# Embedding gate of a decoder block as seven products of halves, with weight sums and half of the output additions done by transfers

## The chip, the core and the metric

The kernel runs on one core of a Trainium2 chip. The engines named below are PE (TensorE, the matrix products), DVE (VectorE), ACT (ScalarE), POOL (GpSimd, which also issues DMA transfers from its own queue) and SP (SyncE, which issues most DMA transfers). The metric is the device time of one execution in microseconds (us), as the median of several runs.

## The reference, cut to what matters

The model is one decoder layer on 512 tokens of width 1024 in float32. The change touches only its last part, the gated per-layer input embedding:

```
x = x + rms_norm(hid @ w_down, g_ffn_post)
ple_gate = sigmoid(rms_norm(x, g_ple_gate) @ w_ple_gate)
ple = rms_norm(p @ w_ple_proj, g_ple_post)
x = x + ple_gate * ple
```

`rms_norm(x, g)` is `x * rsqrt(mean(x*x) + eps) * g`. The product with `w_ple_gate` (1024 by 1024) is called the gate below; `w_down` gives the down product ahead of it.

## The kernel before, in words

**Three matmuls for one product.** Every float32 operand is split into a high part `hi` (a cast on ACT) and a low part `lo` (the source minus `hi`, on DVE). `mm3` (L218 to L224) issues hi·hi, hi·lo and lo·hi into one PSUM bank. `split` (L193 to L197) makes the two parts of an activation. `prep` (L455) does it for a weight piece: SP loads it into a `raw` tile, ACT casts (L480), DVE subtracts (L191, inside `sub`). `weight` (L496) calls `prep` a few pieces ahead of use, and `raw`, `hi` and `lo` have six buffers each.

**Seven products for eight.** The large products ahead of the gate (`rg`, `wo`, `up`, `wd`) are computed in Strassen's manner, in Winograd's form: operands are cut in halves each way, and seven products of half operands stand for eight. Sums of activation halves are formed on DVE and split into `hi` and `lo` again (a "form"). Sums of weight halves are made in DRAM ahead of time, by POOL transfers that add to their destination (`sum_in_dram`, L302 to L313). The products run in the order SERIAL = 1, 2, 5, 6, 3, 7, 4, through `product` (L875), which goes over pieces `q` of the weight and two token tiles `i`.

**The end of the kernel.** The tokens are four tiles (t = 0 to 3) of 128. The last of the down products (number 4) runs its first half for both tiles, then the second half for tile 0 of the pair and for tile 1. `x3_norm` and `x3_add` finish the residual stream of a tile: a square sum on ACT, an inverse root on POOL (L511), a scaled addition on DVE (L1023), then a product with the norm's weight `g_ple_gate` (L1380). Tiles 0 and 1 are finished while PE is still in the down product; tiles 2 and 3 only after it. `x3_tile` transposes a tile on PE (L1034, eight 128 by 128 transposes) and splits the result (ACT L195, DVE L191).

The gate of before is a plain product. For each output half `h` and tile `t`, 24 matmuls of 512 columns (8 blocks of the width by 3) go to a bank of their own, and behind them come the sigmoid (ACT L166, with the tile's `r3` as a scale), a product with the embedding (DVE L1474), an addition of the residual stream (DVE L1475) and a store by SP (L1476). Only the last tile is cut in two parts of 256 columns, each with its own bank. The transposes of tile 2 stand after nine matmuls of tile 1 in the first half, those of tile 3 at that tile's end.

**What sets the order.** PE runs in the order of the code (`manual_schedule`). The other engines' queues are ordered by a scheduler with priorities (`urgent()` raises one). Each engine runs its queue strictly in order: an instruction that waits holds everything behind it.

## Time and profile before

| what | value |
|---|---|
| device time, median of 3 runs | 701.57 us (699.75 to 702.25) |
| profiled execution, from its first to its last instruction | 698.0 us |
| PE busy | 692.4 us, 99% |
| DVE busy | 591.4 us, 85% |
| ACT busy | 453.9 us, 65% |
| POOL busy | 97.1 us, 14% |

The profiled execution is one more execution under the hardware profiler; its own time is known only as its span of 698.0 us. The median of the runs is 3.6 us above that span. Times within the kernel are counted from the span's start. A row of the timeline gives start, duration, engine, line, operation and the tiles written and read; in brackets stand the idle time ahead of it and what ended it. A row of a group gives the number of instructions, their busy time in us and the mean of one in ns, then the idle time of the engine ahead of them.

### The profile page before, as it was taken

What the parts mean: (1) busy time and instruction counts of PE and PEld (TensorE: products, weight loads), DVE (VectorE), ACT (ScalarE), POOL (GpSimd) and SP (SyncE); (2) the same over time, 40 slices, a digit from 0 to 9 for tenths busy, and PEclk for the clock granted to TensorE, in tenths of its full rate; (3) what the DMA queues carried; (4) which work ended last, traced back from release to release, by engine and by line L of the source; (5) the groups of instructions that cost most, each with busy time, mean ns of one, the idle gap of its engine ahead of it and who ended that gap; (6) DMA issues with size and microseconds to landing.
All of it is one profiled execution on the core that took longest, in us unless ns stands there. A gap on an engine that the chain in (4) does not pass through costs nothing.

```text
span 698.0 us, 11598 instructions
## 1 busy us (share of the span) xinstructions
PE 692.4 (99%) x4423; PEld 638.1 (91%) x4423; DVE 591.4 (85%) x772; ACT 453.9 (65%) x693; POOL 97.1 (14%) x123
## 2 busy tenths in 40 slices
...
GB/s 318 408 310 258 251 246 245 264 229 288 261 335 293 301 386 255 346 211 208 115 312 229 191 271 205 202 260 243 173 215 384 241 299 329 343 211 283 29 61 61
DMA packets 67287, 175.71 MB, mean 252 GB/s; under 512 B 6048, under 2 KB 6688, under 8 KB 66848
## 3 DMA queue, kind: packets, MB, share of 16 engines
...
q10 hardware_dynamic: 144, 0.00, 0.0%
...
## 4 chain that ended last, share of the span: by engine, by line
PE 99%; DVE 0%; ACT 0%; issue 0%
PE ps L222 31%; PE ps L223 31%; PE ps L224 31%; PE ps L591 3%; PE ps L1034 1%; PE ps L700 1%; PE ps L241 1%; PE ps L642 0%; ACT t L166 0%; DVE t L1474 0%; DVE t L1475 0%; PE ps L1160 0%; DVE m L233 0%; DVE mhalf L235 0%
## 5 line engine op out<-in xcount | busy, mean ns | idle before, releaser
L191 DVE TENSOR_TENSOR lo<-raw,hi 128x1024 fp32r<-128x1024 f32 (+2 forms) x199 | 230.3, 1183 | 46.1 <-ACT hi L480 29.6
L222 PE MATMUL ps<-A,hi 128*128 128x256 f32 (+1 forms) x672 | 211.9, 315 | 0.0
L224 PE MATMUL ps<-A,lo 128*128 128x256 f32 (+1 forms) x672 | 211.4, 315 | 0.0
L223 PE MATMUL ps<-A,hi 128*128 128x256 f32 (+1 forms) x672 | 211.4, 315 | 0.0
L480 ACT CAST hi<-raw 128x1024 fp32r<-128x1024 f32 (+1 forms) x118 | 118.1, 1012 | 56.7 <-PE ps L224 21.5
L222 PEld LDWEIGHTS ps<-A,hi 128*128 128x128 f32 x672 | 128.2, 191 | 8.0 <-issue 1.0
L224 PEld LDWEIGHTS ps<-A,lo 128*128 128x128 f32 x672 | 128.3, 191 | 6.9
L223 PEld LDWEIGHTS ps<-A,hi 128*128 128x128 f32 x672 | 128.3, 191 | 6.8
L222 PE MATMUL ps<-C,hi 128*128 128x256 f32 x376 | 103.4, 275 | 0.0
L223 PE MATMUL ps<-C,hi 128*128 128x256 f32 x376 | 103.2, 275 | 0.0
L224 PE MATMUL ps<-C,lo 128*128 128x256 f32 x376 | 103.2, 274 | 0.0
L195 ACT CAST hi<-raw 128x1024 fp32r<-128x1024 f32 x75 | 77.8, 1051 | 20.5 <-PE ps L223 12.8
L222 PE MATMUL ps<-hi,A 128*128 128x512 f32 x224 | 85.2, 380 | 0.0
L223 PE MATMUL ps<-lo,A 128*128 128x512 f32 x224 | 84.9, 379 | 0.0
L224 PE MATMUL ps<-hi,A 128*128 128x512 f32 x224 | 84.9, 379 | 0.0
L222 PEld LDWEIGHTS ps<-C,hi 128*128 128x128 f32 x376 | 71.8, 191 | 0.2
L223 PEld LDWEIGHTS ps<-C,hi 128*128 128x128 f32 x376 | 71.8, 191 | 0.1
L224 PEld LDWEIGHTS ps<-C,lo 128*128 128x128 f32 x376 | 71.8, 191 | 0.0
L511 POOL TENSOR_TENSOR s<-s,mhalf 128x1 f32<-128x1 f32 (+1 forms) x21 | 17.4, 829 | 262.6 <-DVE s L528 240.0
L307 POOL DMA_DIRECT2D wdsum<-in_w_down_dram x36 | 33.1, 1055 | 141.3 <-ACT t L1170 62.8
L224 PEld LDWEIGHTS ps<-hi,A 128*128 128x128 f32 x224 | 42.3, 189 | 6.0
L223 PEld LDWEIGHTS ps<-lo,A 128*128 128x128 f32 x224 | 42.4, 189 | 5.9
...
## 6 DMA issues: line engine op xcount, KB each, us to landing
raw<-in_w_up_dram SPq DMA_DIRECT2D x46, 512.0 KB, 5.9
wdsum<-in_w_down_dram POOLq DMA_DIRECT2D x36, 512.0 KB, 7.6
raw<-in_w_in_dram SPq DMA_DIRECT2D x32, 512.0 KB, 8.0
raw<-wdsum SPq DMA_DIRECT2D x24, 512.0 KB, 8.2
raw<-in_w_down_dram SPq DMA_DIRECT2D x18, 512.0 KB, 7.3
wosum<-in_w_o_dram POOLq DMA_DIRECT2D x12, 512.0 KB, 8.7
wdsum<-wdsum POOLq DMA_DIRECT2D x12, 512.0 KB, 6.6
raw<-wosum SPq DMA_DIRECT2D x8, 512.0 KB, 6.1
```

The costliest lines, as they stand in the source:

```text
L191: return V.tensor_tensor(o, a, b, ALU.subtract)
L195: last_copy[0] = ACT.copy(hi, src)
L222: PE.matmul(o, ah, bh, start=start, stop=False, **kw)
L223: PE.matmul(o, ah, bl, start=False, stop=False, **kw)
L224: PE.matmul(o, al, bh, start=False, stop=stop, **kw)
L241: PE.matmul(wps[:, :P], ones, ones, start=True, stop=True)
L307: ins = nc.gpsimd.dma_start(o, i, **kw)
L480: ins = ACT.copy(hi, raw)
L511: last_pow[0] = nc.gpsimd.tensor_tensor(y, v, mhalf[:, :n], ALU.pow).ins.name
L591: PE.matmul(rx[m], a[:, o : o + P], turns(b), start=k == 0 and i == 0, stop=k == KD - 1 and i == 2)
L700: PE.matmul(ps, bd[pr, a, o], turns(b[pr]), start=i == 0, stop=i == 2)
L1034: PE.transpose(ps[:, q * P : (q + 1) * P], a[:, q * P : (q + 1) * P], ident)
```

## The change

The gate becomes seven products of halves in the order 1, 2, 5, 6, 3, 7, 4, each with 24 matmuls of 512 columns (2 pieces, 2 blocks in each, 2 token tiles, 3 matmuls). Products 1 and 2 use token tiles 0 and 1 only; the other five need forms that hold halves of tiles 2 and 3 too.

- **Weight sums.** Two tiles `gsum` in SBUF take weight blocks by SP loads (L1496) and sums by adding POOL transfers into SBUF (L1499). The sums of products 6 and 4 are added to the same tile later, in `prep` (L463), after product 5's, then product 6's, sum has been split.
- **Norm weight.** It is no longer multiplied in by DVE ahead of the transposes. `x3_tile` copies each transposed 128 by 128 block out of PSUM with the weight as a scale (L1412: eight ACT instructions for a tile).
- **Forms.** `g_form` (L1431 and the split at L196) makes the form of each product, for single tiles in products 1, 2 and 5.
- **Outputs.** Four of the eight output pieces are stored first as plain residual stream (L1399) and get gate times embedding added by a POOL transfer into DRAM (L1527). The others are added on DVE as before. The last one is again in two parts of 256 columns, now in one bank.
- **Embedding.** Its loads and its eight products with the norm weight (L1460 before, L1486 now) stand ahead of the last down product.

```diff
-    for h in range(2):
-        for kp in range(4):
-            plan(("wpg", kp, h), rows2(w_ple_gate, kp, h))
+    for f in SERIAL:
+        for q in range(pieces["wg"]):
+            plan(("wg", f, q), piece_of("wg", f, q))
...
+        if key[0] == "wg" and key[1] > 3:
+            _, f, q = key
+            t = gsum[f == 7][:, 2 * q : 2 * q + 2, :]
+            if f in (6, 4):
+                nc.gpsimd.dma_start(t, block_of("wg", {6: 3, 4: 2}[f], q), accum_op=ALU.add)
+            ready[key] = parts_of(D)
+            split(*(v.rearrange("p (k c) -> p k c", k=2) for v in ready[key]), t)
...
     def x3_add(t):
...
-            for h in range(2):
-                x3n[t, h] = nq[t // 2][:, 2 * (t % 2) + h, :]
-                x3_last[0] = V.tensor_tensor(x3n[t, h], res[h], gq[:, 2 + h, :], ALU.mult).ins.name
...
-    def x3_tile(t):
-        xq = hquad(F32R)
+    def x3_tile(t, into=(None, None)):
         for h in range(2):
-            ps = transposed(x3n[t, h])
-            x3t[t, h] = xq[:, 2 * h, :], xq[:, 2 * h + 1, :]
+            ps = transposed(x3[t // 2][:, 2 * (t % 2) + h, :], into[h])
             with urgent():
-                split(*x3t[t, h], ps)
-
+                for k in range(4):
+                    g = gple[:, 4 * h + k : 4 * h + k + 1]
+                    ACT.activation(xt3[h][:, k, t * P : (t + 1) * P], ps[:, k * P : (k + 1) * P], AF.Identity, scale=g)
...
+        for i in tiles:
+            part = (lambda u: u) if i is None else (lambda u: u[:, :, i * P : (i + 1) * P])
+            if a is not None:
+                V.tensor_tensor(part(v), part(a), part(b), op)
+            split(part(gform[f][:, 0]), part(gform[f][:, 1]), part(v))
...
+        act(row(o), back(src), AF.Sigmoid, scale=r3[t])
+        V.tensor_tensor(row(o), row(o), part(ple[t // 2][:, i, :]), ALU.mult)
+        o_dram = part(out[t * P : (t + 1) * P, h * S : (h + 1) * S])
+        if (t, h) in OUT_LAST:
+            V.tensor_tensor(row(o), row(o), part(x3[t // 2][:, i, :]), ALU.add)
+            nc.sync.dma_start(o_dram, row(o))
+        else:
+            nc.gpsimd.dma_start(o_dram, row(o), accum_op=ALU.add)
+
+    gz, g11, g12 = ([bank(), bank()] for _ in range(3))
+    for q in product("wg", g_lhs, 1, gz, True, tail=2):
+        with urgent():
+            ACT.copy(g11[q - 2], gz[q - 2])
+    for q in product("wg", g_lhs, 2, g11, False, tail=2):
+        x3_tile(q, dd)
+        with urgent():
+            g_form(5, (q - 2,))
+        finish(q - 2, 0, g11[q - 2])
+    g5 = wpool.tile([P, 2, S], F32, tag="sum", name=nm("sum"), bufs=1)
+    g_form(6)
+    for q in product("wg", g_lhs, 5, dd, True, tail=2):
+        with urgent():
+            ACT.copy(g5[:, q - 2], dd[q - 2])
+    g_form(3)
+    for q in product("wg", g_lhs, 6, gz, False, tail=2):
+        with urgent():
+            V.tensor_tensor(g12[q - 2], g5[:, q - 2], gz[q - 2], ALU.subtract)
+    g_form(7)
+    for q in product("wg", g_lhs, 3, g12, False, tail=2):
+        finish(q - 2, 1, g12[q - 2])
+    g_form(4)
+    for q in product("wg", g_lhs, 7, gz, False, tail=2):
+        with urgent():
+            V.tensor_tensor(g5[:, q - 2], g5[:, q - 2], gz[q - 2], ALU.subtract)
+    halves_of = ((0, HALF), (HALF, S))
+    for q in product("wg", g_lhs, 4, gz, False, tail=2, parts=halves_of):
+        if q == 2:
+            for t in (2, 3):
+                finish(t, 1, g5[:, t - 2])
+            finish(2, 0, gz[0])
+        else:
+            a, b = halves_of[q - 3]
+            finish(3, 0, gz[1][:, a:b], a, b)
```

Three places of the engines' queues follow, as the built programs have them; what an instruction waits for stands in brackets (DMASW: a POOL transfer, DMAHW: an SP transfer).

ACT from the first sigmoid of the gate on, before: `h` are the transposed tiles 2 and 3, `hi` the weights of the second output half.

```order
L166 ACTIVATE t_7165<-ps_7167,r_6934 128x512 [waits PE_49]
L516 ACTIVATE rb,s_7155<-C_6908 128x512 [waits DVE_49,Activation_49]
L195 CAST h_7208<-ps_7209 128x512 [waits PE_49]
L195 CAST h_7208<-ps_7216 128x512 [waits PE_49]
L516 ACTIVATE rb,s_7157<-C_6908 128x512 [waits DVE_49,Activation_49]
L166 ACTIVATE t_7196<-ps_7198,r_7020 128x512 [waits PE_49]
L195 CAST h_7242<-ps_7243 128x512 [waits PE_49]
L195 CAST h_7242<-ps_7250 128x512 [waits PE_49]
L480 CAST hi_7262<-raw_7260 128x1024 [waits DMAHW4_49]
L480 CAST hi_7274<-raw_7272 128x1024 [waits DMAHW5_49]
```

ACT at the same place in the change: `h_7035` and `h_7036` take the transposed blocks, `A_7265` is the form of product 5 (tile 2, then tile 3), `hi_7233` and `hi_7280` are the weight sums of product 6, read from `gsum` (`h_7038`).

```order
L167 ACTIVATE t_7269<-ps_7194,r_6933 128x512 [waits PE_49]
L1412 ACTIVATE h_7035<-ps_3028,gple 128x128 [waits PE_49]
L1412 ACTIVATE h_7035<-ps_3028,gple 128x128 x3
L1412 ACTIVATE h_7036<-ps_6165,gple 128x128 [waits PE_49]
L1412 ACTIVATE h_7036<-ps_6165,gple 128x128 x3
L1412 ACTIVATE h_7035<-ps_3028,gple 128x128 [waits PE_49]
L1412 ACTIVATE h_7035<-ps_3028,gple 128x128 x3
L196 CAST A_7265<-C_7037 128x4x128 [waits DVE_49]
L1412 ACTIVATE h_7036<-ps_6165,gple 128x128 [waits PE_49]
L1412 ACTIVATE h_7036<-ps_6165,gple 128x128 x3
L196 CAST hi_7233<-h_7038 128x1024 [waits DMASW4_49]
L196 CAST hi_7280<-h_7038 128x1024 [waits DMASW5_49]
```

The next row of the change is the cast of product 5's form for tile 3 (`A_7265` again). It stands behind two weight casts that each wait for an adding transfer; before, nothing between the sigmoids waited for a transfer except the last two rows.

POOL over the same stretch of the change: the inverse roots (L522), and between them the adding transfers of weights (L463) and of outputs (L1527).

```order
L522 TENSOR_TENSOR s_7166<-s_7164,mhalf 128x1 [waits DVE_49,Pool_49]
L463 DMA h_7038<-in_w_ple_gate_dram 128x2x512 [waits DMASW0_49,DMASW4_49,DVE_49,Activation_49]
L522 TENSOR_TENSOR s_7176<-s_7174,mhalf 128x1 [waits DVE_49,Pool_49]
L463 DMA h_7038<-in_w_ple_gate_dram 128x2x512 [waits DMASW2_49,DMASW5_49,DVE_49,Activation_49]
L522 TENSOR_TENSOR s_7188<-s_7186,mhalf 128x1 [waits DVE_49,Pool_49]
L1527 DMA out_dram<-t_7269 128x512 [waits DMAHW3_49,DMASW6_49,DVE_49]
L463 DMA h_7038<-in_w_ple_gate_dram 128x2x512 [waits DMASW7_49,DMASW4_49,DVE_49]
L463 DMA h_7038<-in_w_ple_gate_dram 128x2x512 [waits DMASW5_49,DVE_49]
```

Before, POOL had only inverse roots there. Each of the first two weight transfers now waits for DVE, which has to finish the `lo` part of product 5's sum in the same tile first.

PE at the change's very end: `ps_7193` is the bank of the last output piece, first its columns 0 to 255, then 256 to 511.

```order
L223 MATMUL ps_7193<-hi_7426,A_7440 128x256
L224 MATMUL ps_7193<-lo_7427,A_7440 128x256
L225 MATMUL ps_7193<-hi_7426,A_7440 128x256
L223 MATMUL ps_7193<-hi_7399,A_7440 128x256 [waits Activation_49]
L224 MATMUL ps_7193<-lo_7400,A_7440 128x256
```

The second part waits for ACT, which reads the first part from the same bank; before, the two parts were in two banks (`ps_7438` and `ps_7467`) and the second waited for nothing but PE itself.

139 lines of the change are left out of this document (82 added, 57 removed).

## The prediction

> **What bounds the kernel now.** I read the busy shares and the chain of waits on the page first, and then stretches of the end in the view by windows (columns: stretch, its length, busy time of PE, PEld, DVE, ACT and POOL, granted clock, DMA share, GB/s).
>
> ```profile
> PE 692.4 (99%) x4423; PEld 638.1 (91%) x4423; DVE 591.4 (85%) x772; ACT 453.9 (65%) x693; POOL 97.1 (14%) x123
> ...
> PE 99%; DVE 0%; ACT 0%; issue 0%
> ```
>
> ```profile
> 640.00:650.00 10.00, 10.00 (x56) 8.88 (x55) 10.00 (x17) 6.93 (x12) 1.88 (x2) 1.00 0.65 226
> 650.00:660.00 10.00, 10.00 (x52) 8.83 (x51) 8.91 (x17) 7.13 (x16) 1.51 (x3) 1.00 0.00 0
> 660.00:670.00 10.00, 10.00 (x52) 8.83 (x51) 9.53 (x16) 5.28 (x7) 0.92 (x1) 1.00 0.15 54
> 690.00:698.00 8.00, 3.46 (x31) 3.27 (x30) 2.03 (x5) 0.95 (x2) 0.00 (x0) 0.87 0.19 68
> ```
>
> PE is the bound, and the chain is PE alone: matmuls saved shorten the kernel one for one, as long as everything that they read is there. But from 640 to 660 DVE is 89 to 100% busy and ACT 69 to 71%. So the forms that the change asks for there must find room on two engines that have little. The whole sum is matmuls saved less new PE waits; none of the terms behind (a) can be a gain, since PE waits for nothing from 640 to 670.
>
> **(a) Matmuls.** The PE groups of the gate, and PE's timeline around tile 2's transposes (start, duration):
>
> ```profile
> L222 PE MATMUL ps<-hi,h 128*128 128x512 f32 x56 | 21.4, 382 | 0.0
> ...
> L222 PE MATMUL ps<-hi,h 128*128 128x256 f32 x16 | 4.4, 275 | 0.0
> ```
>
> ```profile
> 655.54 0.38 PE L224 MATMUL ps<-hi,h 128*128 128x512 f32 x1
> ...
> 656.83 0.38 PE L224 MATMUL ps<-hi,h 128*128 128x512 f32 x1
> 657.05 1.04 PE L1034 MATMUL ps<-ident,h 128*128 128x128 f32 x8
> 657.84 0.46 PE L222 MATMUL ps<-hi,h 128*128 128x512 f32 x1
> ```
>
> Matmuls overlap, so starts are counted: seven steps from 655.54 to 657.05 make 0.2157 us each. L222, L223 and L224 have 56 whole and 16 half matmuls each: 3 × (56 + 16/2) = 192 whole ones. The change has 7 × 24 = 168. That saves 24 × 0.2157 = **5.2 us**. The gate starts 33 matmuls ahead of 657.05, at 649.9. Eight transposes take 657.84 − 657.05 = 0.8, as many as before.
>
> **Prices for the rest**, from the groups of ACT and DVE after 600 us and from ACT's timeline:
>
> ```profile
> L166 ACT ACT_TABLE_LOAD x1 | 1.3, 1283 | 0.0
> ...
> L166 ACT ACTIVATE t<-ps,r 128x256 f32<-128x256 f32 x2 | 0.9, 473 | 4.1 <-PE ps L224 4.1
> ```
>
> ```profile
> L191 DVE TENSOR_TENSOR lo<-raw,hi 128x1024 fp32r<-128x1024 f32 x22 | 26.5, 1223 | 3.5 <-ACT hi L480 3.4
> L1460 DVE SCALAR_TENSOR_TENSOR A<-A,rp,h 128x512 f32<-128x512 f32 x8 | 5.8, 743 | 0.0
> ...
> L191 DVE TENSOR_TENSOR h<-ps,h 128x512 fp32r<-128x512 f32 x8 | 5.2, 680 | 0.0
> L1380 DVE TENSOR_TENSOR C<-C,C 128x512 f32<-128x512 f32 x4 | 2.7, 685 | 0.0
> ```
>
> ```profile
> 639.83 2.92 ACT L480 CAST hi<-raw 128x1024 fp32r<-128x1024 f32 x3
> 642.66 1.06 ACT L195 CAST h<-ps 128x512 fp32r<-128x512 f32 x2
> 645.45 0.60 ACT L516 ACTIVATE rb<-ps 128x512 f32<-128x512 f32 x1 [1.72 <-PE ps L224]
> ...
> 646.03 0.58 ACT L195 CAST h<-ps 128x512 fp32r<-128x512 f32 x1
> ...
> 661.36 0.69 ACT L166 ACTIVATE t<-ps,r 128x512 f32<-128x512 f32 x1 [1.98 <-PE ps L224]
> 661.95 1.06 ACT L195 CAST h<-ps 128x512 fp32r<-128x512 f32 x2
> ```
>
> A cast of a weight occupies ACT 0.95 (three in 2.92), a square 0.6 (645.45 to 646.03). A block copy of 128 columns isn't in the trace. L166 takes 0.69 for 512 columns and 0.473 for 256, so by the same slope 0.365 for 128. Two neighbours overlap by 0.1 (661.36 + 0.69 against 661.95), which leaves 0.27 for one copy in a row. Bounds: 0.17, a quarter of the 0.69, and 0.37 without overlap. I take 0.27; the 256-column row is the nearest.
>
> **(b) Tile 1's transposes**, in the chain of waits of before (start, duration):
>
> ```profile
> 645.33 0.87 PE ps L1034 x8
> ```
>
> Tiles 0 and 1 now share two banks, and tile 1's transposes (PE comes to the second bank's four 0.4 after these 645.33, at 645.7) wait for tile 0's copies. In front of these copies DVE gets the eight embedding products (0.743 each) in place of the two L1380 (0.685 each); with what of that lies in gaps, ACT, which came to the split at 642.66, comes some 1.1 later, at 643.8. Eight copies (2.1) and a half cast among them (0.52) end at 646.5: **+0.8** (0 with copies of 0.17, 1.3 with 0.37).
>
> **(c) Form of product 5, tile 2.** From 646.9 ACT has, without a gap in its queue, 8 squares (4.8), tile 1's 8 copies (2.1), 2 half casts (1.0), 3 weight casts (2.85), 2 bank copies (1.0), the table load (1.2 net of an overlap of 0.1) and a sigmoid (0.6): 13.55, up to 660.4. Then come tile 2's eight copies and four of tile 3's, which end at 663.85 (tile 3's transposes wait for the banks). The form's difference (0.69 on DVE) is ready by then, and the half cast ends at 664.9. PE has done products 1 and 2 and the transposes at 649.9 + 0.8 + 48 × 0.2157 + 2 × 0.8, with 0.4 in the bank wait and latencies, = 663.05. It waits 1.9 for `hi`. For `lo`, DVE does product 7's difference (1.2 wide) ahead, another 0.65: **+2.55** (2.0 to 3.0).
>
> **(d) Form of product 5, tile 3.** Its cast stands on ACT behind the casts of `hi_7233` and `hi_7280`, which wait for adding transfers on POOL. The nearest rows: DVE's last norm addition, POOL's root behind it, four earlier transfers in POOL's queue of the kind that makes the sums (L307; those at 119.69 and 122.47 were released by those of 112.12 and 113.47), and the plain loads of SP (size, median us to landing).
>
> ```profile
> 655.24 1.41 DVE L1023 SCALAR_TENSOR_TENSOR C<-t,s,C 128x512 f32<-128x512 f32 x2 [0.66 <-POOL s L511]
> ```
>
> ```profile
> 658.07 0.92 POOL L511 TENSOR_TENSOR s<-s,mhalf 128x1 f32<-128x1 f32 x1 [2.87 <-DVE s L528]
> ```
>
> ```profile
> 112.12 1.06 POOL L307 DMA_DIRECT2D wosum<-in_w_o_dram  x1 [6.75 <-DMA wosum<-wosum]
> 113.47 1.04 POOL L307 DMA_DIRECT2D wosum<-in_w_o_dram  x1 [0.29 <-DMA wosum<-wosum]
> 119.69 0.52 POOL L307 DMA_DIRECT2D wosum<-wosum  x1 [5.18 <-DMA wosum<-in_w_o_dram]
> 122.47 0.52 POOL L307 DMA_DIRECT2D wosum<-wosum  x1 [2.25 <-DMA wosum<-in_w_o_dram]
> ```
>
> ```profile
> raw<-in_w_ple_gate_dram SPq DMA_DIRECT2D x8, 512.0 KB, 4.0
> ```
>
> Tile 3's two norm additions, at 655.24 before, end near 658.0 with the later DVE of (b); the `lo` parts of product 5's sums (1.15 apart) end at 659.1 and 660.3. The first transfer is issued at 659.2; the second comes behind a root (0.75), at 661.0. Transfers of 512 KB in this queue were over 7.6 and 9.0 us after issue (112.12 to 119.69, 113.47 to 122.47), under load; a plain load takes 4.0. After issue at 661.0 that gives 668.6, 670.0 and 665.0. The window 650 to 660 shows a DMA share of 0.00, so I take 668.0, a little under the nearest row; bounds 665.0 and 671 (9.0, and another transfer's issue of 1.04). Behind it stand the weight's cast (0.95) and the form's (0.62): `hi` at 669.7. PE is ready at 663.05 + 2.55 + 12 × 0.2157 = 668.2 and waits 1.5, then for `lo` 0.9 more: **+2.4** (1.1 to 5.5). ACT is free for the second weight cast at 666.8: a landing ahead of that leaves only 1.1, and each us later costs one. As the landing is a fixed moment, what (b) or (c) save is partly lost here again.
>
> **(e) Form of product 6.** Behind tile 3's cast ACT has a sigmoid (0.6), a copy (0.5), three weight casts (2.85) and the form's cast (1.05): 5.0, against 3.5 on PE (12 matmuls and the 0.9): 1.4. On DVE the form's `lo` follows three more long operations, 1.2 later: **+2.6** (2.0 to 3.0). Behind it, the forms of 3, 7 and 4 come in time: a product is 5.2 of PE, and each brings one cast and one `lo` with its difference (1.05; 2.4) and at most two weight casts (2.0).
>
> **(f) The last output.** Its second half reads a bank that ACT is reading: 0.47 for the sigmoid and two latencies, **+0.7**; with the sigmoids' rows **+0.8** (0.6 to 1.5). From the last matmul to the end nothing changes.
>
> **At no cost:** SP's loads of the weight blocks and the stores of the residual stream go out while the down products run; the additions to DRAM have at least 8 us until the end. The sums of product 4 are needed some 10 us after their issue. Were these late, (f)'s upper bound takes it.
>
> **Sum:** −5.2 + 0.8 + 2.55 + 2.4 + 2.6 + 0.8 = +4.0 (bounds +0.5 to +9.1). The profiled execution of 698.0 becomes 702.0; the median of the runs, 3.6 higher, becomes **705.6 us**.
>
> **Rivals.**
> - *A, the sum above*, +3 to +6.
> - *B, the sums land early*, as the plain load: (d) 1.1, the sum +2.7; with copies of 0.17 (b) is 0 and (c) 1.6, the sum +0.9. About 703.4. For it: no other transfer loads the engines. Against: both transfers quoted took 7.6 us or more. The Trainium skill ("DMA: Bandwidth & Descriptors", the section on the anatomy of one DMA on the SWDGE path) gives about 2.0 us and bytes over 436 GB/s for such a transfer, an estimate of 3.2 us here, by which (d) would be 1.1; the 7.6 us of the trace speak against it, though under load.
> - *C, the sums land late*, from 670.0 on, some 0.6 later in the middle: (d) 5.0, the sum +6.6, about 708.2. For it: the row that gives 9.0, and the output addition that POOL issues at 663.8 on the same queue. By the Trainium skill ("TensorE: Matmul & The Clock Gate", Part 1) the clock falls to half after an idle window of about 3.4 us; the row of 690 to 698, with 4.5 us idle and 0.87, agrees, and an estimate by that page adds up to 1.7 us in C.
> - *D, faster:* ACT stays ahead of PE. If ACT reached the first form 4 us earlier, at 660 (squares and weight casts moved into its idle 1.7 at 645 and the like), and the sums landed by 664, then (c), (d) and (e) would go together and (b) too: −5.2 + 0.8 = −4.4, 697.2. It decides at 663.05, when PE is ready. Against it: 13.55 us of rows in that queue, and DVE full.
> - That matmuls are not saved is excluded: the changed order has 168.
>
> **How the numbers follow.** A 0.58, B 0.22, C 0.14, D 0.06. 0.5% is 3.5 us, about what a measurement of this kernel can tell from no change. Below 698.1 lies most of D: faster 0.05. From 698.1 to 705.1 lie B, the rest of D and a third of A: 0.42. The rest of A and C are slower: 0.53. The range leaves out D and the upper half of C: its low end is the lower bound of the sum less the runs' own spread below their median (1.8 at most, half taken), 701.2; its high end lies a little under the upper bound, 709.0.
>
> **What would show it.** Right: about 168 gate matmuls; PE idle of 2 to 3 us ahead of each of the first matmuls of product 5 (both tiles) and of product 6, released by ACT and DVE; ACT idle for about 2 us before the second of two casts near 668, released by a POOL transfer; 0.7 idle between the two last halves. Wrong: landings under 5 us (B), over 10 us (C), no PE idle in product 5 (D), or waits in a place not named here, first of all a late sum of product 4.

## The result, and the profile after

The kernel with the change takes **708.75 us** (median of six runs, 706.90 to 716.39) against 700.70 us for the kernel before beside it: a ratio of 1.0142 (95% interval 1.0105 to 1.018). A second measurement on another chip gave 708.67 against 700.61 us, ratio 1.0098 (1.0068 to 1.0129). So the change costs about 8 us. The prediction had 4.0 us, in the right direction and half the size.

The profiled execution is the longest of the six, with a span of 714.6 us. Busy shares and the shares of the chain of waits, on the page:

```profile
PE 696.7 (97%) x4387; PEld 637.0 (89%) x4387; DVE 601.8 (84%) x777; ACT 472.8 (66%) x737; POOL 110.1 (15%) x135
...
PE 66%; DVE 13%; DMA 8%; ACT 7%; issue 4%; POOL 1%; SPq 1%; ACTq 0%; DVEq 0%; POOLq 0%
```

The 24 matmuls are saved; in instructions it is 36 (4423 to 4387), since the gate has 24 of half width where it had 48. But the chain, PE alone before, now runs a third of its length through other engines. The view by windows over the end says where (columns as in the prediction: busy time of PE, PEld, DVE, ACT and POOL, granted clock, DMA share, GB/s):

```profile
630.00:640.00 10.00, 7.67 (x36) 6.41 (x35) 9.54 (x14) 6.95 (x13) 3.59 (x3) 0.99 0.96 251
640.00:650.00 10.00, 10.00 (x44) 8.55 (x43) 5.92 (x9) 1.88 (x4) 3.00 (x3) 0.84 1.07 359
650.00:660.00 10.00, 8.26 (x35) 6.55 (x34) 6.44 (x11) 9.97 (x29) 1.08 (x2) 0.85 0.77 175
660.00:670.00 10.00, 10.00 (x47) 8.73 (x46) 8.12 (x12) 9.38 (x22) 1.34 (x3) 0.98 0.00 1
670.00:680.00 10.00, 8.04 (x39) 6.43 (x37) 6.27 (x10) 9.37 (x23) 4.33 (x6) 0.87 0.77 131
680.00:690.00 10.00, 7.58 (x27) 5.75 (x26) 9.11 (x10) 6.50 (x8) 2.69 (x3) 0.84 0.78 134
```

Three things stand here. PE has idle time in four of the six stretches. The granted clock is 0.84 to 0.87 in four, where it was 1.00 before. And ACT, which is full from 650 to 680, has only 1.88 of work in the ten microseconds ahead of that: it was waiting while its work piled up. PE's waits in this stretch, from its timeline (start, duration, line, and in brackets the idle time and what ended it):

```profile
639.38 0.45 PE L223 MATMUL ps<-hi,A 128*128 128x512 f32 x1 [2.33 <-DVE sum L1473]
...
654.67 0.66 PE L1051 MATMUL ps<-ident,C 128*128 128x128 f32 x4 [0.84 <-ACT h L1412]
656.23 0.66 PE L1051 MATMUL ps<-ident,C 128*128 128x128 f32 x4 [0.90 <-ACT h L1412]
...
675.87 0.48 PE L223 MATMUL ps<-hi,A 128*128 128x512 f32 x1 [1.30 <-ACT A L196]
677.22 0.67 PE L225 MATMUL ps<-hi,A 128*128 128x512 f32 x1 [0.66 <-DVE A L192]
...
685.79 0.48 PE L223 MATMUL ps<-hi,A 128*128 128x512 f32 x1 [1.87 <-ACT A L196]
687.05 0.48 PE L225 MATMUL ps<-hi,A 128*128 128x512 f32 x1 [0.56 <-DVE A L192]
...
708.61 0.38 PE L223 MATMUL ps<-hi,A 128*128 128x256 f32 x1 [0.56 <-ACT t L167]
```

In order: the last down product waits for an addition of the previous one (`sum`), then come tile 1's transposes (step b), the forms of product 5 (c) and of product 6 (e), and the last output (f). The first of them is in no step of the prediction; it sits in the stage ahead of the gate. DVE's timeline ahead of it:

```profile
617.48 2.08 DVE L1486 SCALAR_TENSOR_TENSOR h<-h,rp,C 128x512 f32<-128x512 f32 x3 [1.39 <-DMA h<-pled]
...
638.56 0.68 DVE L1473 TENSOR_TENSOR sum<-sum,ps 128x512 f32<-128x512 f32 x1
```

L1486 is the embedding's product with the norm weight, eight times 0.7 us. Behind the first three there is next to no idle time on DVE until the `sum` that PE waits for.

Then DVE itself stops, for 4 us, and ACT for 8. Three timelines (POOL, DVE, ACT):

```profile
645.47 2.48 POOL L1499 DMA_DIRECT2D h<-in_w_ple_gate_dram  x2 [9.88 <-DMA h<-in_w_ple_gate_dram]
647.50 1.04 POOL L522 TENSOR_TENSOR s<-s,mhalf 128x1 f32<-128x1 f32 x1
```

```profile
648.58 1.41 DVE L1037 SCALAR_TENSOR_TENSOR C<-t,s,C 128x512 f32<-128x512 f32 x2 [4.07 <-POOL s L522]
```

```profile
649.42 0.63 ACT L527 ACTIVATE rb<-C 128x512 f32<-128x512 f32 x1 [8.12 <-DVE C L1037]
```

Tile 1's inverse root (L522) stands on POOL behind two adding transfers, and these hold POOL's queue for 9.88 us until SP's loads of the same tile are there. DVE's norm addition waits for the root, ACT's square for that, and tile 0's block copies stand behind the square. No cast of ACT waits for a weight in this stretch.

The two numbers that the prediction had to estimate without a row are there now: a group, and the DMA issues of the stretch from 600 us on (size, median us to landing):

```profile
L1412 ACT ACTIVATE h<-ps,gple 128x128 f32<-128x128 f32 x32 | 9.2, 382 | 0.5 <-PE ps L1051 0.5
```

```profile
raw<-in_w_ple_gate_dram SPq DMA_DIRECT2D x6, 512.0 KB, 12.6
```

A block copy lasts 0.382 by itself (the estimate was 0.365), and five in a row on ACT's timeline take 1.38, 0.25 apart (the estimate 0.27). SP's loads of the gate's weights, 4.0 before, take 12.6. The adding transfers of the sums (L463) landed 6.4 us after issue in the median, 5.8 to 7.5.

**How the length adds up.** A wait costs more than its idle time: the matmul ahead of it overlaps with nothing (0.38 long instead of a step of 0.2157, 0.16 more), and the step behind it is about 0.1 longer (676.05 to 676.37 in a timeline below). That makes 0.27 a wait. And the clock drops; the 2-us windows behind the first wait:

```profile
638.00:640.00 2.00, 0.62 (x3) 0.57 (x4) 2.00 (x4) 1.26 (x3) 0.00 (x0) 0.96 1.10 266
640.00:642.00 2.00, 2.00 (x6) 1.60 (x5) 2.00 (x4) 1.30 (x2) 0.00 (x0) 0.50 1.09 255
642.00:644.00 2.00, 2.00 (x8) 1.63 (x7) 2.00 (x3) 0.00 (x0) 0.00 (x0) 0.69 1.08 332
```

The clock is 0.5 for about 3.4 us: 2 × (0.04 + 0.50 + 0.31) = 1.7 us are lost. In this execution that happens four times: behind the `sum`, behind tile 1's transposes and behind each pair of form waits. In the second measurement's profiled execution (span 708.5) it happens twice, each time for 3.4 us again. In seven of the experiments below a stretch lasts twice as long, 6.8 us (one is shown under "All that had seemed to help together"). Counted from the kernel before (698.0), in us; the last two columns are experiments of the next section:

| term | forecast | change, span 714.6 | change again, span 708.5 | without four adding transfers, span 702.0 |
|---|---|---|---|---|
| (a) 24 matmuls | −5.2 | −5.2 | −5.2 | −5.2 |
| (b) tile 1's transposes | +0.8 | 1.74 | 2.04 | 0 |
| (c) product 5, tile 2 | +2.55 | 1.96 | 1.96 | 2.27 |
| (d) product 5, tile 3 | +2.4 | 0 | 0.76 | 0.81 |
| (e) product 6 | +2.6 | 2.43 | 2.02 | 2.62 |
| (f) last output | +0.8 | 0.56 | 0.56 | 0.57 |
| waits of the down products | none | 2.33 | 2.55 | 0.90 |
| 0.27 for each wait | none | 2.2 (8) | 2.4 (9) | 2.2 (8) |
| half clock, 1.7 each | none | 6.8 (4) | 3.4 (2) | 0 |
| sum | +4.0 | +12.8 | +10.5 | +4.2 |
| measured | | +16.6 | +10.5 | +4.0 |

The sums meet the spans of the last two, but for a wait of 0.74 at 9 us in the execution of 708.5, which isn't counted. The long execution has further waits between 211 and 277 us (0.40, 0.80, 1.07) and in its first 10 us (0.16, 0.96), far from anything that the change touches; with 0.27 for each they make another 4.7, and the sum 17.5, 0.9 over what was measured.

### The profile page after: what moved, and what is told of

It reads as the page before. It is cut to its first block, busy times and chain, and to the rows that moved or that the text cites. A ratio compares the mean times of both kernels' runs of the same rounds, so it can differ in the third digit from the quotient of the medians.

```text
span 714.6 us, 11618 instructions
## 1 busy us (share of the span) xinstructions
PE 696.7 (97%) x4387; PEld 637.0 (89%) x4387; DVE 601.8 (84%) x777; ACT 472.8 (66%) x737; POOL 110.1 (15%) x135
## 4 chain that ended last, share of the span: by engine, by line
PE 66%; DVE 13%; DMA 8%; ACT 7%; issue 4%; POOL 1%; SPq 1%; ACTq 0%; DVEq 0%; POOLq 0%
PE ps L225 21%; PE ps L223 21%; PE ps L224 21%; DVE lo L192 3%; DMA parts<-hi 3%; PE ps L602 3%; DMA h<-in_w_ple_gate_dram 2%; ACT hi L495 2%; ACT m L167 1%; DVE A L192 1%; DVE m L740 1%; ACT t L167 1%; DMA h<-pled 1%; ACT hi L196 1%; DMA m<-in_rows_dram 1%
## 5 line engine op out<-in xcount | busy, mean ns | idle before, releaser
L192 DVE TENSOR_TENSOR lo<-raw,hi 128x1024 fp32r<-128x1024 f32 (+2 forms) x197 | 227.9, 1182 | 46.7 <-ACT hi L495 25.7
L495 ACT CAST hi<-raw 128x1024 fp32r<-128x1024 f32 (+1 forms) x116 | 115.6, 1011 | 52.4 <-PE ps L225 14.6
L223 PE MATMUL ps<-hi,A 128*128 128x512 f32 (+1 forms) x284 | 110.1, 388 | 6.1 <-ACT A L196 3.2
L225 PE MATMUL ps<-hi,A 128*128 128x512 f32 (+1 forms) x284 | 110.0, 387 | 2.3 <-DVE A L192 2.3
L224 PE MATMUL ps<-lo,A 128*128 128x512 f32 (+1 forms) x284 | 109.4, 385 | 0.0
L196 ACT CAST hi<-raw 128x1024 fp32r<-128x1024 f32 x75 | 77.7, 1053 | 19.8 <-PE ps L224 12.0
L223 PEld LDWEIGHTS ps<-hi,A 128*128 128x128 f32 x284 | 55.4, 195 | 15.1 <-ACT A L196 3.8
L225 PEld LDWEIGHTS ps<-hi,A 128*128 128x128 f32 x284 | 55.2, 194 | 11.5 <-DVE A L192 3.5
L224 PEld LDWEIGHTS ps<-lo,A 128*128 128x128 f32 x284 | 55.2, 194 | 8.0
L522 POOL TENSOR_TENSOR s<-s,mhalf 128x1 f32<-128x1 f32 (+1 forms) x21 | 19.3, 918 | 245.6 <-DVE s L539 223.2
```

What stands on the lines that cost most here:

```text
L192: return V.tensor_tensor(o, a, b, ALU.subtract)
L196: last_copy[0] = ACT.copy(hi, src)
L223: PE.matmul(o, ah, bh, start=start, stop=False, **kw)
L224: PE.matmul(o, ah, bl, start=False, stop=False, **kw)
L225: PE.matmul(o, al, bh, start=False, stop=stop, **kw)
L495: ins = ACT.copy(hi, raw)
```

## The experiments

Each kernel was timed beside the kernel before on the same chip; medians in us.

**The change once more**, to see what varies.

> The changed kernel once more, to see which of the first profile's PE waits belong to it and which to that execution. Theory (waits and clock): the four groups of waits in the gate and ahead of it (for the sum of down product 7, 2.3 us; tile 1's transposes, 1.7; product 5's form, 2.0; product 6's form, 2.4) are there again within 1 us, and behind each group PE's matmuls run for about 3.4 us at half the clock, 1.7 to 2.0 us lost each time; the three waits of 0.4 to 1.1 us before 300 us and those of the first 10 us are not there; span 705 to 709. Rival (the sum on record, waits alone): the granted clock is 1.00 in all stretches but the last and the span is 702.

708.67 (706.22 to 710.96). The runs follow the mean clock: spans of 704.5 and 705.2 at a clock of 1.0, 705.9 at 0.997, 708.5 at 0.995, 707.9 and 709.2 at 0.993. So the spread of these six runs goes with the clock, and at full clock the kernel is still 6.5 to 7.2 us above the 698.0 of before. In the first measurement the clock doesn't explain all of it: there, runs at a clock of 0.995 had spans of 707.0 and 711.6. Here the wait for `sum` was the longer one and no half clock followed (PE's timeline, then the window around it):

```profile
635.83 0.45 PE L223 MATMUL ps<-hi,A 128*128 128x512 f32 x1 [2.55 <-DVE sum L1473]
```

```profile
634.00:640.00 6.00, 4.17 (x19) 3.70 (x20) 6.00 (x9) 2.57 (x4) 0.00 (x0) 1.00 0.97 267
```

Product 5's first pair of waits is the same as in the first profile, 1.30 and 0.66, and no half clock follows it either (1.00 from 670 to 676).

**The embedding products back** behind tile 1's norm and behind product 5's forms; their loads stay early.

```diff
-    for t in range(NT):
-        for h in range(2):
-            v = ple[t // 2][:, 2 * (t % 2) + h, :]
-            V.scalar_tensor_tensor(v, v, rp[t], gq[:, 2 + h, :], ALU.mult, ALU.mult)
...
+        if a == 0:
+            ins = V.scalar_tensor_tensor(v, v, rp[t], gq[:, 2 + h, :], ALU.mult, ALU.mult)
+            behind(ins, x3_done[1] if h == 0 and t < 2 else form5[0])
```

> The eight embedding products go back behind the norm of tile 1 (four of them behind product 5's forms); the loads stay early. Theory: the wait for the sum of down product 7 (2.3 us) and the half clock behind it (1.8) go, tile 1 is finished earlier, and the kernel is 3 to 5 us faster than the changed one, some 704. Rival: the embedding's early loads and the other traffic make the weights late, not DVE's work; then the wait stays and the time is within 1 us of the changed kernel's.

705.98 (705.84 to 712.03), ratio 1.0093 (1.0056 to 1.0131). The wait for `sum` is 0.52, with the loads still early, so the products made it. The median is 2.7 less than the change's on the same chip, but two of the six runs took 712.03, and by the ratios (1.0093 against 1.0098) the two kernels can't be told apart. The edit also changes POOL's order: tile 1's root now starts at 630.38, ahead of three of the four adding transfers (634.24 to 637.40), so both delays of the change are out of this kernel.

**Only the embedding moved**, in the kernel before: the same loads and eight products ahead of the last down product, and nothing else of the change.

```diff
+    for t in range(NT):
+        for h in range(2):
+            v = ple[t // 2][:, 2 * (t % 2) + h, :]
+            V.scalar_tensor_tensor(v, v, rp[t], gp[:, h, :], ALU.mult, ALU.mult)
     for q in down_product(4, zd, False, head=3, tail=DOWN_TAIL):
```

> The kernel before with the embedding's loads and products alone moved ahead of the last down product. Theory (DVE's work moved into a full stretch): PE waits 1 to 3 us for a DVE result near 637, and with the half clock behind it the kernel is 2 to 5 us slower than before. Rival: DVE had room there, no wait, within 0.5 us of before.

706.26 (704.88 to 709.21), ratio 1.0074 (1.0048 to 1.0101). This part alone costs 5.6 us, although it adds no work. PE's timeline and the clock around its first long wait:

```profile
636.36 0.45 PE L222 MATMUL ps<-hi,A 128*128 128x512 f32 x1 [2.90 <-DVE sum L1428]
...
640.46 0.48 PE L224 MATMUL ps<-hi,A 128*128 128x512 f32 x1 [0.84 <-DVE A L191]
...
651.88 1.23 PE L1034 MATMUL ps<-ident,C 128*128 128x128 f32 x8 [1.65 <-DVE C L1380]
```

```profile
636.00:640.00 4.00, 3.26 (x14) 2.56 (x14) 4.00 (x6) 0.00 (x0) 0.00 (x0) 1.00 0.48 140
```

The first is the same wait as in the change, and 2.90 us of idle stay without a half clock behind them. It isn't the whole cost: PE also waits 0.47 for DVE at 602, 0.84 for a low part (L191), and 1.65 at tile 1's transposes for L1380. The four idle times (5.86) and 0.27 for each make 6.9, and this execution (704.9) is 6.9 longer than that of before.

**What a wait costs by itself.** The kernel before with four PE waits put into the gate: PE transposes a block that ACT copies one to five times.

```diff
+                if (h, t) in held:
+                    ACT.copy(rb, ps)
+                    for _ in range(held[h, t] - 1):
+                        ACT.copy(rb, rb)
+                    wait_ps = bank()
+                    PE.transpose(wait_ps[:, :P], rb[:, :P], ident)
```

> The kernel before with four PE waits put in by chains of 1, 2, 3 and 5 ACT copies ahead of a transpose, behind four products of the gate (waits of about 0.8, 1.4, 2.0 and 3.1 us, 7 us together). Theory (a wait beyond about 1.3 us halves the clock for some 3.4 us): granted clock 1.00 behind the first, half behind the others for about 3.4 us each, and the kernel is 7 + 3 x 1.8 = 12 us slower than before. Rival (a wait costs itself): 1.00 throughout and 7 us slower.

711.77 (711.05 to 712.83), 11.2 above before; the profiled execution, of 711.1, is 13.1 above that of before. PE's timeline, and windows around the second, third and fourth wait:

```profile
673.24 0.33 PE L1480 MATMUL ps<-ident,rb 128*128 128x128 f32 x1 [0.73 <-ACT rb L1476]
680.58 0.33 PE L1480 MATMUL ps<-ident,rb 128*128 128x128 f32 x1 [1.83 <-ACT rb L1478]
688.57 0.45 PE L1480 MATMUL ps<-ident,rb 128*128 128x128 f32 x1 [2.48 <-ACT rb L1478]
699.53 0.48 PE L1480 MATMUL ps<-ident,rb 128*128 128x128 f32 x1 [3.78 <-ACT rb L1478]
```

```profile
680.00:684.00 4.00, 3.42 (x17) 3.02 (x18) 1.38 (x2) 0.52 (x2) 0.00 (x0) 1.00 0.17 66
...
688.00:690.00 2.00, 1.43 (x4) 1.26 (x5) 0.77 (x2) 0.51 (x1) 0.00 (x0) 0.66 0.15 55
690.00:692.00 2.00, 2.00 (x6) 1.55 (x6) 0.00 (x0) 0.00 (x0) 0.00 (x0) 0.50 0.20 76
...
700.00:702.00 2.00, 2.00 (x12) 2.00 (x11) 0.00 (x0) 0.00 (x0) 0.00 (x0) 0.50 0.03 10
```

Full clock behind the waits of 0.73 and 1.83, half behind those of 2.48 and 3.78. The idle times make 8.8, two stretches of half clock 3.4 and four times 0.27 another 1.1: 13.3, against the 13.1 measured.

**POOL's queue.** The second pair of adding transfers behind tile 1's root, else the change.

```diff
-                    nc.gpsimd.dma_start(t[:, 2 * q2 : 2 * q2 + 2, :], block_of("wg", a, q2), accum_op=ALU.add)
+                    ins = nc.gpsimd.dma_start(t[:, 2 * q2 : 2 * q2 + 2, :], block_of("wg", a, q2), accum_op=ALU.add)
+                    if t is gsum[1]:
+                        behind(ins, last_pow[0])
```

> The changed kernel with one order changed on POOL: the two adding transfers of product 7's sums stand behind tile 1's inverse roots, not ahead of them. In both profiles of the change DVE waited 2.6 to 4.1 us for that root, which stood behind a transfer that waited 8.6 to 9.9 us for SP's loads. Theory (POOL's queue makes tile 1 late): this DVE wait falls under 1 us and PE's two waits at tile 1's transposes (2.0 us together, with half a clock behind them) go or fall under 1 us: 2 to 4 us faster than the changed kernel. The wait for the sum of down product 7 (2.3 to 2.6) stays, since it lies ahead. Rival (DVE's embedding products alone make tile 1 late): tile 1's waits stay and the time is within 1 us of the changed kernel's.

707.40 (705.98 to 708.28), ratio 1.0106 (1.0093 to 1.0119). On PE tile 1's transposes wait 0.46 instead of about 2, and DVE waits 0.76 for the root instead of 4.07:

```profile
648.82 0.66 PE L1051 MATMUL ps<-ident,C 128*128 128x128 f32 x4 [0.46 <-ACT h L1412]
```

DVE's wait for the root is shown to come from POOL's queue. The edit also issues two of the four transfers later, and SP's loads of the gate's weights land after 7.4 us instead of 10.7 to 12.6, so at tile 1's transposes the two effects aren't told apart. The time, 1.3 less than the change on another chip, lies within the intervals.

**The embedding scaled where it is computed**, near 330 us, with the root first.

```diff
+        for h, o in enumerate(outs):
+            V.scalar_tensor_tensor(o, o, rp[t], g_ple[h], ALU.mult, ALU.mult)
+            nc.sync.dma_start(pled[t * P : (t + 1) * P, h * S : (h + 1) * S], o)
```

> Both delays taken away: the embedding products are done far earlier, where the embedding is computed (its tiles are scaled before they are stored), and tile 1's roots stand ahead of product 7's adding transfers. Theory: no PE wait for the sum of down product 7 and none at tile 1's transposes; what remains are the forms of products 5 and 6 (about 2 us each) and the last output (0.56), with half a clock behind the two forms: waits 4.5 and clock 3.6 against 5.2 saved, so 2 to 4 us slower than before, some 703.5. Rival (ACT alone is too full for the forms): tile 1's waits stay at 1 to 2 us even so, and the time is that of the kernel with the embedding back, 706.

708.19 (707.14 to 709.44). The wait for `sum` falls to 0.52 and that of tile 1 to nothing, but four new waits stand between 326 and 348 us, 3.5 together. DVE has no room there either.

**Eight useless matmuls** ahead of product 5 and of product 6, with the embedding back; they keep PE busy while it would wait.

```diff
+        for _ in range(n):
+            PE.matmul(g12[0], a, b, start=True, stop=True, skip_group_check=True)
```

> The kernel with the embedding products back, and in it eight matmuls without a use (1.7 us, into a bank that is free) ahead of product 5 and ahead of product 6, where PE waited 1.6 and 2.0 us for forms; the order on all other engines is the same. Theory (the half clock follows from PE's idleness): the granted clock is 1.00 behind both places, and the kernel is 2 to 4 us faster than the one with the embedding back though it does 16 matmuls more, some 702.5. Rival (a wait costs itself, the clock is nothing): the same time within 0.7 us, or up to 0.8 more where the matmuls are longer than the waits.

708.50 (703.77 to 711.50): in the median no gain, 2.5 more than with the embedding back on another chip. The clock stays at 1.00 at both forms, and the fastest run of a version of the change so far is among these. But the profiled execution has 1.74 of waits at tile 1's transposes, with half clock behind them, and they begin at a weight (ACT):

```profile
644.94 1.04 ACT L495 CAST hi<-raw 128x1024 fp32r<-128x1024 f32 x1 [3.67 <-DMA raw<-in_w_ple_gate_dram]
```

**One form earlier.** With the embedding back, first product 5's form ahead of two sigmoids and of product 6's weight casts; then product 6's form ahead of the casts of products 3 and 7.

```diff
+    for ins in late_sig:
+        behind(ins, last_copy[0].ins.name)
+    for hi, lo in six:
+        behind(hi, last_copy[0].ins.name)
+        behind(lo, last_sub[0].ins.name)
```

> The kernel with the embedding products back, and on ACT the first two sigmoids (with the table load) and the two casts of product 6's sums stand behind product 5's forms of both tiles. Theory (ACT's queue in order makes the forms late: what stands ahead of a form's cast is the wait): PE's waits for product 5's forms (1.6 and 0.3 us in the kernel with the embedding back) go or fall under 0.5 us. Those of product 6 (2.0) stay or grow by up to 1. Time 1 to 3 us less than with the embedding back, 703 to 705. Rival (the transposes or the norm of tiles 2 and 3 set the moment): the waits stay within 0.3 us.

712.67 in the median of five runs (707.92 to 714.80); a sixth took 718.66. Product 5 waits only 0.80, and product 6 takes it all: 3.21 + 1.25, then 1.48 in a later product. ACT again waited for a weight, 5.20, and tile 1's transposes 4.07.

```diff
+            if key[:2] == ("wg", 3):
+                behind(ins, form6["hi"])
```

> The kernel with the embedding products back, and the casts and lo parts of the weights of products 3 and 7 stand behind product 6's form. Theory: the wait for product 6's form (1.33 and 0.69 us) goes or falls under 0.7 us together; product 5's waits stay; 1.5 to 3.5 us less than with the embedding back where the half clock goes too. Rival (DVE's form of the difference, not the casts, is late): the wait stays over 1.3 us; or a wait of the same size comes up ahead of product 3, whose weights are now later.

711.75 (710.37 to 713.81). Product 6 waits 0.39 + 0.68; product 3, which had no wait, now 0.84 + 0.98. In both, a wait that is taken from one form turns up at the next. Not all of the added time is the forms': here too ACT waited 4.93 for a weight and tile 1's transposes 2.86 + 0.90, which with the embedding back alone had no wait.

**Both forms first**, all embedding products behind them, the root first, the last product in another order.

```diff
+    for ins in embs:
+        behind(ins, form6["lo"])
```

> Both orders together, all eight embedding products behind product 6's form, tile 1's roots ahead of product 7's adding transfers, and the last product in the order first part of tile 3, tile 2, second part of tile 3. Theory: of the waits only single ones under 1 us are left (sum of down product 7 about 0.5), the clock stays at 1.00 up to the last us, and the kernel is 1 to 4 us faster than before, some 698. Rival (DVE and ACT are too full in total; a wait removed comes up later): waits of 3 us or more together behind product 5, and a time of 702 or more.

712.49 (711.38 to 713.69). Waits of 0.91, 1.81, 3.21 + 0.26, 3.27 + 1.11 and 0.87: no better than one form alone.

**Less work for ACT.** The norm weight is left out of the gate, so that one copy of 512 columns takes the place of four of 128; product 6's weight casts stand behind product 5's first form.

```diff
-                for k in range(4):
-                    g = gple[:, 4 * h + k : 4 * h + k + 1]
-                    ACT.activation(xt3[h][:, k, t * P : (t + 1) * P], ps[:, k * P : (k + 1) * P], AF.Identity, scale=g)
+                ACT.copy(xt3[h][:, :, t * P : (t + 1) * P], ps.rearrange("p (k c) -> p k c", k=4))
```

> The kernel with the embedding products back, without the norm weight in the gate (left out of the result): each half of a transposed tile is copied by one ACT instruction of 512 columns in place of four of 128, and the casts of product 6's sums stand behind product 5's first form. ACT has 32 x 0.25 - 8 x 0.52 = 3.9 us less to do between 644 and 665. Theory (ACT is full from tile 0's copies to product 6's form, and the waits in the gate are its excess): PE's waits for the forms of products 5 and 6 (3.8 us together with the embedding back) fall by 2 us or more, and the time by 2 to 5 with the half clocks. Rival (DVE, or weights that land late, set the forms): they fall by less than 0.7 us.

707.59 (704.81 to 707.96). The form waits are 4.2, as with the embedding back alone (4.2). ACT's timeline:

```profile
646.98 1.04 ACT L497 CAST hi<-raw 128x1024 fp32r<-128x1024 f32 x1 [5.12 <-DMA raw<-in_w_ple_gate_dram]
```

So shorter copies alone didn't shorten the form waits; but as a weight held ACT for 5.12 us and tile 1's transposes waited 2.21, this run doesn't decide what the copies' length is worth.

**Half of the copies of tiles 2 and 3 on DVE**, in the order of the last kernel.

```diff
+                    if h == 0 or t < 2:
+                        ACT.activation(o, i, AF.Identity, scale=g)
+                    else:
+                        V.tensor_scalar(o, i, g, None, ALU.mult)
```

> The kernel with the embedding products back, where DVE makes half of the block copies of tiles 2 and 3 (eight of 128 columns), and the casts of product 6's sums stand behind product 5's first form. ACT has 2 us less, DVE about as much more. Theory (ACT is full, DVE has room from 660 on): the waits for the forms of products 5 and 6 fall by 1 to 2 us together. Rival (both are full): they stay within 0.5 us or grow at product 6.

712.24 (706.63 to 714.62). Tile 1's transposes waited 3.35 + 0.43, product 5 2.23 + 0.34, product 6 0.92 + 1.63.

**The sums made early in DRAM**, as for the products ahead of the gate, and loaded by SP; the embedding back.

```diff
-    sum_in_dram(chain_of(sums_of("rg"), sums_of("wo"), sums_of("up")), None)
+    sum_in_dram(chain_of(sums_of("rg"), sums_of("wo"), sums_of("up"), sums_of("wg")), None)
```

> The kernel with the embedding products back, with the gate's weight sums made in DRAM far ahead (behind those of the other products on POOL) and loaded by SP like any weight: no loads and adding transfers into SBUF from 618 to 675. Theory (the traffic of 620 to 650 makes the gate's weights late: SP's loads of w_ple_gate took 10 to 14 us to land in the changed kernels, 4.0 before, and ACT waits for them with tile 0's copies behind): these loads land in 4 to 7 us, ACT's wait ahead of tile 0's copies goes, PE's waits at tile 1's transposes are 0 in the profile and the runs are closer together; 1 to 3 us less than with the embedding back, unless the transfers of 200 to 300 us hold up something there. Rival (the landing is no cause; ACT is late by its own work): the waits at tile 1's transposes and the spread of the runs stay.

726.01 (722.55 to 731.23). In the gate the loads take 4.5 and tile 1 has no wait, but PE has three new waits early (4.59 at 212, 4.96 at 222 and 4.37 at 248). They make 13.9 us by themselves, so this kernel can't tell what late weights cost in the gate.

**All outputs added by DVE** and stored by SP, as before the change; the embedding back.

```diff
-    OUT_LAST = ((2, 1), (3, 1), (2, 0), (3, 0))
+    OUT_LAST = tuple((t, h) for t in range(4) for h in range(2))
```

> The kernel with the embedding products back, and all eight outputs added by DVE and stored by SP as before: no stores of the residual stream at 624 to 645 (1 MB) and no adding transfers at the end, four more DVE additions (2.8 us). Theory (traffic): the loads of w_ple_gate land 1 to 4 us earlier and the waits at tile 1's transposes are gone; on the other side DVE's additions stand among the forms: within 1 us of the kernel with the embedding back. Rival (the stores are nothing, DVE is full): 1 to 3 us slower.

705.77 (703.83 to 711.59), ratio 1.0084 (1.0055 to 1.0114), beside 705.98 with the output transfers. They cost nothing that can be measured.

**Without the four adding transfers** (L1499) that make the sums of products 5 and 7, on top of the last kernel: those two products use one block of each sum.

```diff
-            for t, a in zip(gsum, (0, 3)):
-                for q2 in range(2):
-                    nc.gpsimd.dma_start(t[:, 2 * q2 : 2 * q2 + 2, :], block_of("wg", a, q2), accum_op=ALU.add)
```

> The version with the embedding products back and all outputs added by DVE, without the four adding transfers that make the weight sums of products 5 and 7 ahead of the gate (so products 5 and 7 multiply by one block of the sum alone, and the result is not the reference's); their plain loads stay. Theory 'transfers': the adding transfers of 512 KB share the engines with SP's loads of the first weights of the gate, which is why these land 10 to 14 us after issue and not 4. Without them the loads land in 4 to 7 us, ACT's wait for raw is under 1.5 us, tile 1's transposes wait under 0.5 us, and the median falls from 705.8 by 1 to 2.5 us, to 703.3 to 704.8. Rival 'plain loads': the two plain loads of weights into the sum tiles and the loads of the residual stream are enough to delay them; the loads stay at 9 us or more and the median stays within 1 us of 705.8. By both the waits at the forms of products 5 and 6 (about 4 us together) stay.

704.33 (703.18 to 706.02), ratio 1.0063 (1.0049 to 1.0078). The DMA issues from 600 us on:

```profile
raw<-in_w_ple_gate_dram SPq DMA_DIRECT2D x6, 512.0 KB, 4.2
```

4.2 us, against 12.4 with these transfers: they are what holds the weights up. ACT doesn't wait for a weight, and tile 1's transposes don't wait. In the profile of the last kernel they didn't either; ACT's waits for a weight stand in six other profiles with the embedding back and these transfers, the longest of each 1.29 to 5.20. PE's waits are those of the forms, at a clock of 1.00 throughout:

```profile
665.33 0.48 PE L223 MATMUL ps<-hi,A 128*128 128x512 f32 x1 [1.88 <-ACT A L196]
...
666.41 0.48 PE L225 MATMUL ps<-hi,A 128*128 128x512 f32 x1 [0.39 <-DVE A L192]
...
670.31 0.48 PE L225 MATMUL ps<-hi,A 128*128 128x512 f32 x1 [0.81 <-DVE A L192]
673.65 0.48 PE L223 MATMUL ps<-hi,A 128*128 128x512 f32 x1 [0.92 <-ACT A L196]
676.05 0.48 PE L225 MATMUL ps<-hi,A 128*128 128x512 f32 x1 [1.70 <-DVE A L192]
676.37 0.38 PE L223 MATMUL ps<-hi,A 128*128 128x512 f32 x1
```

**All that had seemed to help together**: the embedding back, outputs by DVE, the root first; nothing left out.

```diff
+                    if t is gsum[1]:
+                        behind(ins, last_pow[0])
```

> Everything that had helped put together: the embedding products back, all outputs added by DVE, and the second pair of adding transfers behind tile 1's inverse root on POOL. If the gains of the parts add up (root 1.2 us against the change, the embedding 2.7, the outputs 0.2), the median is 708.7 less 4.1 = 704.6 us, still above before by 0.6 percent, with waits of about 4 us left at the forms. If the root's gain and the embedding's gain are the same wait at tile 1, it stays at 705.8. Below 701, which would make it level with before, only if the form waits fall too, which neither theory expects.

704.84 (703.17 to 706.62) against 699.87, ratio 1.0063 (1.005 to 1.0075). It is the best complete version, 5.0 above before where the change is 8.0 above, and only 0.5 above the kernel without the four transfers on the same chip. Its waits: 0.51 for `sum`, none at tile 1, 2.24 and 0.83 at product 5, 2.61 at product 6, 0.57 at the end. With two of the four transfers behind the root, SP's loads land after 7.4. Behind product 6's waits the clock is halved for 6.8 us (in four windows of 2 us, 2 × (0.28 + 0.50 + 0.50 + 0.43) = 3.4 us are lost):

```profile
674.00:676.00 2.00, 0.46 (x1) 0.46 (x2) 2.00 (x3) 0.50 (x1) 0.00 (x0) 0.72 1.12 222
676.00:678.00 2.00, 2.00 (x6) 1.55 (x6) 2.00 (x3) 0.21 (x1) 0.00 (x0) 0.50 0.31 108
...
680.00:682.00 2.00, 2.00 (x7) 1.61 (x6) 1.79 (x2) 0.00 (x0) 0.00 (x0) 0.57 0.00 0
```

Counted like the table, −5.2, the waits of 6.8, seven times 0.27 and 3.4 make 6.9, and the execution (704.9) is 6.9 above before. No version beats the kernel before.

**Short copies and early weights**: the kernel without the four transfers, and one ACT copy of 512 columns for four of 128 (again the norm weight is left out of the gate). In the second kernel the two first sigmoids also stand behind product 5's form.

```diff
-                for k in range(4):
-                    g = gple[:, 4 * h + k : 4 * h + k + 1]
-                    ACT.activation(xt3[h][:, k, t * P : (t + 1) * P], ps[:, k * P : (k + 1) * P], AF.Identity, scale=g)
+                ACT.copy(xt3[h][:, :, t * P : (t + 1) * P], ps.rearrange("p (k c) -> p k c", k=4))
```

> The kernel without the four adding transfers (704.33, loads of the gate's weights 4.2 us), and now also without the norm weight of the gate, so that one ACT copy of 512 columns takes the place of four of 128. Theory 'ACT is behind': at tile 2's transposes ACT still had 12 block copies to do (3.4 us, from 660.56 to 664), which become three copies of about 0.5 us; so the wait at product 5's first form falls from 1.88 to under 0.5 us, the one at product 6 from 2.62 to under 1.5, and the median from 704.3 to about 701. Rival 'the loop between PE, ACT and DVE': a form needs transposes, copy, difference, cast and lo part one after the other whatever the load of ACT, with DVE's output operations ahead of it; product 5's waits stay over 1.5 us together, product 6's over 2 us, and the median stays above 703.

706.37 (705.77 to 706.71), ratio 1.0095 (1.0078 to 1.0112): slower than with the long copies. ACT's timeline, then PE's:

```profile
660.28 1.06 ACT L1410 COPY h<-ps 128x512 f32<-128x512 f32 x2
663.70 1.04 ACT L196 CAST hi<-h 128x1024 fp32r<-128x1024 f32 x1 [2.35 <-DMA h<-in_w_ple_gate_dram]
666.26 1.04 ACT L196 CAST hi<-h 128x1024 fp32r<-128x1024 f32 x1 [1.52 <-DMA h<-in_w_ple_gate_dram]
```

```profile
668.36 0.79 PE L223 MATMUL ps<-hi,A 128*128 128x512 f32 x1 [5.05 <-ACT h L1410]
```

Neither theory had this. ACT is indeed done with its copies some 2.6 us sooner, at 661.3, and then it meets the two weight casts that wait for the adding transfers of `prep` (L463): 2.35 and 1.52, with the cast of the form and tile 3's last copies behind them. PE waits 5.05 in one piece, and the clock is at 0.50 from within this wait until 672, 6.8 us in all.

```diff
+    for ins in late_sig:
+        behind(ins, last_copy[0].ins.name)
```

> As the one with short copies, and the two sigmoids of the first half's tiles 0 and 1 (with their products and additions on DVE behind them) wait for product 5's form. Theory 'ACT is behind': about the same as with short copies alone, within 1 us. Rival 'the loop': the table load (1.28 us), the sigmoid (0.6) and three DVE operations of 0.7 leave the way of product 5's form, so its waits fall below 1 us here and not with short copies alone; they turn up again at product 6, where the sigmoids then stand.

707.35 (707.14 to 708.33). The same: ACT waits 3.19 and 1.14 for the transfers, PE 5.63.

## Why the prediction was half right

The direction came out, the size did not. In the second profile the prediction's own terms make 2.1 of the 10.5 us; the other 8.4 are costs that it had put at nothing: the waits of the down products (2.55), 0.27 for each wait (2.4) and half clock (3.4).

**Right: (a), (c), (e), (f).** The matmuls are saved and eaten up by the forms. Where nothing else disturbs (the last column of the table), PE waits 2.27 at product 5 for `hi` and then `lo`, 2.62 at product 6 and 0.57 at the last output, against 2.55, 2.6 and 0.8. Some of this closeness is luck. In (c) ACT's twelve copies end there at 663.96, as forecast (663.85); but the difference was not "ready by then": it stands behind two output operations on DVE, and ACT idles 0.70 for it. In (e) the parts are 0.92 and 1.70 where 1.4 and 1.2 were forecast (and the prediction's own 5.0 less 3.5 makes 1.5), while the change itself has 1.87 and 0.56.

**Mis-sized: (d),** 2.4 forecast, 0 to 0.81 measured. The prediction had the two adding transfers issued at 659.2 and 661.0 and the second landed at 668.0. In the kernel without the four transfers, where the rest of the stretch runs as forecast, POOL issued them at 658.88 and 660.20, and ACT cast both sums at 666.19 without a wait. The landing took 6.3 us in the median there, not 7. Earlier issue by 0.8 and a landing shorter by 0.7 put the second sum at about 666.5 (an estimate from that median), just ahead of ACT, which starts its second cast near 667.1. So the outcome of rival B came about for this term, but not for B's reason: no transfer of L463 landed in under 5.5 us in any run, against B's 4.0 or 3.2. The change's rise in time has another source. The mechanism was real all the same: with the embedding back ACT waits 0.84 for the sum, and with short copies it gets to the sums first and waits 2.35 and 1.52 for them.

**Wrong: "eight embedding products … some 1.1 later" in (b), and "at no cost".** The prediction priced the moved embedding where it stands ahead of tile 0's copies, and never asked who else waits for DVE between 617 and 640. It is PE, in the down product ahead of the gate, for product 7's `sum`: 2.33 to 2.55 us. The experiment that moves nothing but the embedding has this wait (2.90), with 2.96 of others, and costs 5.6 us; moving the products back leaves 0.52 of it. The rows were there to see: DVE at 100% from 640 to 650 in before said that this work had no slack, and the stretch ahead of it, which wasn't opened, has little more:

```profile
630.00:640.00 10.00, 10.00 (x48) 8.74 (x48) 9.28 (x13) 4.54 (x11) 0.54 (x1) 1.00 0.88 299
```

**Wrong by omission: two queues.** SP's loads and the adding transfers on POOL were taken as free because they start while the down products run. The four adding transfers (L1499) each wait for a load of SP, and in the change two of them hold POOL for 9.88 us (8.55 in the second profile), with tile 1's root behind them. DVE waits 4.07 (2.58) for that root, ACT's idle time of 8.12 ahead of tile 0's copies ends only behind it, and tile 1's transposes wait 1.7 to 2.0 instead of (b)'s 0.8. The transfers also run beside the loads of the gate's first weights, which land after 10.7 to 12.6 us instead of 4.0. In the change no cast waits for this; with the embedding back, where the root comes first, ACT waits for a weight in six profiles, the longest of each 1.29 to 5.20. For the first, DVE's wait for the root falls from 4.07 to 0.76 when the root is moved; for the second, the landing falls to 4.2 without the transfers. How much time each is worth is not shown: the order of POOL and the landing changed together when the root was moved, and with the embedding back, leaving out the transfers gains 0.5 against the best version on the same chip.

**Wrong by omission: what a wait costs.** The sum added idle times only. In the two profiles of the change eight or nine waits lose another 0.27 each, 2.2 to 2.4, and half clock takes 1.7 behind four groups of them in one profile and behind two in the other. The clock had been put into rival C alone, as one drop of up to 1.7. The Trainium skill ("TensorE: Matmul & The Clock Gate", Part 1) says that the window in which activity is counted is free-running, about 3.4 us long. The traces agree: the stretches of half clock last 3.4 or 6.8, and the same idle time is sometimes punished and sometimes not (the pair of 1.30 and 0.66 in one profile of the change but not in the other; 2.33 yes, 2.55 and 2.90 no). By the same page of the Trainium skill the clock falls after at least one idle window; waits of 2.33 and 2.48, and pairs as short as 0.84 + 0.90, were enough here.

**Why no single repair that was tried helped the forms.** ACT's copies and the adding transfers of L463 come in within a few microseconds of each other. Without the four early transfers, ACT is last with the long copies (1.88 at product 5, no wait for a transfer); with the short ones the transfers of L463 are (5.05). A form that is put ahead hands its wait to the next one. What a version with short copies and sums that are there earlier would take is open; no run had both.
